# A hybrid attention and state-space layer: two attention gates computed by a third Strassen pair, and earlier steps around it

## Chip, cores and metric

The kernel runs on one core of a Trainium2 chip. The metric is the device time of one execution in microseconds (us); of the kernel before, three runs gave 857.27, 859.77 and 859.24 us, median 859.24. One further execution was taken by the hardware profiler; every row quoted below of the kernel before is from that one.

Engines are named as in the profile: PE is TensorE (matmuls), PEld its weight loads, DVE VectorE, ACT ScalarE, POOL GpSimd, SP the engine whose queue issues the DMAs. L259 is line 259 of the kernel.

## The reference

One layer works on T = 1088 tokens (1024 of a prompt, 64 of a sample) with a model width of 1024. One projection of the normalized input gives the queries, keys and values, two gates `z`, the state-space input `u`, and two merging gates `g`:

```python
xn = rmsnorm(h, norm_gain)
z = xn @ w_in
...
ya = (attn * jax.nn.silu(z_attn)) @ w_o_attn
ys = (ssm * jax.nn.silu(z_ssm)) @ w_o_ssm
merged = jax.nn.sigmoid(g_attn) * ya + jax.nn.sigmoid(g_ssm) * ys
h = h + merged @ w_out
h = h + jax.nn.sigmoid(h @ w_ple_gate) * (p @ w_ple_proj)
```

`attn` is a sliding-window attention, `ssm` a diagonal complex recurrence over the tokens with a gelu and a gated unit behind it. The change concerns `g_attn` (1024 columns of `w_in`, eight units of 128, called m = 0 to 7 here), `z_ssm` (four units), and the time at which the last rounds of the recurrence run.

## The kernel before

**Data.** Tiles hold 128 rows (features) by 1088 columns (tokens) in float32. Each float32 product is made of three matmuls (L259, L260, L261): both operands are split into a high and a low part (`hl_split`: ACT's copy L1158 and DVE's subtraction L162). 43 slots of SBUF are handed out and given back by the program as it is written; a step that needs a slot waits until the last reader of its former content is done. All loads and stores stand in SP's one queue, in program order.

**Clock.** PE's products are written out in one long order, and everything else hangs on a hand-made clock: `pump` is called once after each half of a plain product and once after each half of a Strassen product, and fires what `at(step, ...)` or `later(n, ...)` planned for that step. The tables `ROUND_AT`, `OUT_AT`, `BACK_AT`, `X_AT` and `RING_AT` are such steps. The framework then fixes the order in each engine; what is issued through `first` comes ahead of other work that is ready.

**Stages around the change** (steps in brackets):
- OA [120 to 144]: the last four output tiles of the attention product, four k each, three token blocks of 384, 384 and 320 (`BLK`). ACT copies them out of the banks (L173).
- Plain gates m = 4 to 7 [144 to 168]: eight k each over the same three blocks, so 72 matmuls a unit. DVE multiplies by the token scale RS, ACT takes tanh (L1339), DVE adds 1 and multiplies by the OA tile, and `pa_out` stores the result to DRAM.
- zB [168 to 196]: two pairs of units, each pair by a Strassen scheme (`seven`): seven products of four k over two halves of 544 tokens, in sub-blocks of 272 columns, so 7 x 4 x 3 x 2 = 168 matmuls a pair. `sink` adds the products up on ACT and DVE, and `z_late` finishes a half.
- gB [196 to 252]: four pairs, the same way; then the rest of the layer.

Strassen's products need sums of the quarters of x (S1 to S4 of the weights, T1 to T4 of x): `x_load` brings two tiles of x back from DRAM, three steps before `x_sums` scales them on ACT (L1304) and makes the sums and their splits on DVE and ACT; `x_t1` makes the last one's split later. The weights pass through a ring of four pieces: `rload` loads a unit of `w_in` into a slot, `make` splits a piece into the ring. `ring_start` begins that (steps 136 and 143).

**Rounds.** The recurrence runs in eight rounds of four groups. For a round r, `s_load` brings its inputs, `s_rot` makes a table of rotations (DVE and POOL, L728 among its lines), `s_wb` transposes on PE (L746) and has ACT copy the result out (L747), `s_state` makes the state's input on PE (L789), reading that copy, and rotates and scans it on DVE and POOL (L805), `s_state2` finishes the state (L825 to L827), and `s_out` makes the output on PE (L839, L840), which ACT copies (L841) and SP stores (L844). `ROUND_AT` plans `s_wb` and `s_state`, with the other parts at fixed distances, and `OUT_AT` plans `s_out`. `s_back` reads the output of a quarter of the rounds back for the gelu, at `BACK_AT`.

Of the kernel before, what the change touches and what calls it, by code (L numbers as in the profile page):

```python
# [16 lines left out]
AF = mybir.ActivationFunctionType  # L17
AX = mybir.AxisListType
MUL, ADD, SUB = ALU.mult, ALU.add, ALU.subtract
# [17 lines left out]
ENG = dict(tab="VG", e="V", cf="VG", rot="VG", r8="GGGV", unrot="VG", rotadd="VVG", rope="VVVG", ropeadd="GGV", ropec="VG",  # L37
           gelu="V", norm="V", w="V", gate="VG", glu="GGGV", mg="VVG", pa="V", h="V", acc="V",
           y="VVVG", z="V", ph="VVG", xs="V", ws="V", rs="VG", ms="V", hq="G", zz="GV", tcp="AV")
BACK_AT = (176, 186, 196, 206)  # L40
ROUND_AT = (32, 40, 50, 73, 86, 103, 121, 140)
OUT_AT = (41, 54, 62, 81, 98, 113, 137, 150)
SLOT = 1096
MANUAL = False
AHEAD = 400
BLK = [(0, 384), (384, 384), (768, 320)]
BLK2 = [(0, 416), (416, 416), (832, 256)]
HT = T // 2
RAWS = 3
RING_AT = (136, 143)  # L50
RING = 4
X_AT = (148, 151, 154, 158)

SEVEN = [("A11", "B11", "a", 1), ("A12", "B21", "b", 1), ("S2", "T2", "a", 0), ("S3", "T3", "c", 1),
         ("S1", "T1", "a", 0), ("S4", "B22", "a", 0), ("A22", "T4", "c", 0)]
# [79 lines left out]
def emit(nc, tc, a, es, dbg=None):  # L135
# [7 lines left out]
    S = Slots(sp, NSLOT)  # L143
# [7 lines left out]
    zb_dram = dp.tile([4, P, T], F32, name="zb_dram")  # L151

    V, G, A, PE, DMA = nc.vector, nc.gpsimd, nc.scalar, nc.tensor, nc.sync
# [13 lines left out]
    def stt(o, x, s, y, op0, op1):  # L167
        V.scalar_tensor_tensor(o, x, s, y, op0, op1)  # L168

    def first(f, *x, **k):  # L170

        with tc.high_priority(AHEAD):
            f(*x, **k)  # L173
# [7 lines left out]
    def ett(key, o, x, y, op):  # L181
        (nc.gpsimd if eng(key) == "G" else nc.vector).tensor_tensor(o, x, y, op)  # L182
# [36 lines left out]
    def wget():  # L219
        i = wi["get"]  # L220
        wi["get"] += 1
        if wi["split"] <= i:
            wsplit()
        if wi["split"] == i + 1:
            wsplit()
        return S.ap(whs[i % 2][0]), S.ap(whs[i % 2][1])
# [12 lines left out]
    def at(i, f, *args):  # L239
        plan.setdefault(i, []).append((f, args))  # L240
# [22 lines left out]
    def gemm(w, off, ops, blk, pumps=True):  # L263

        c0, cn = blk
        ps = gbank()[:, :cn]
        nk = len(ops)
        for k, (xh, xl) in enumerate(ops):
            ws = slice(off + P * k, off + P * k + P)
            mm3(ps, w[0][:, ws], w[1][:, ws], S.ap(xh)[:, c0:c0 + cn], S.ap(xl)[:, c0:c0 + cn],  # L270
                k == 0, k == nk - 1)
            if pumps and k == nk // 2 - 1:
                pump()
        if pumps:
            pump()
        return ps, slice(c0, c0 + cn)
# [6 lines left out]
    RS = S.ap(rsb)  # L283
# [378 lines left out]
    V, vtt, stt = V_, vtt_, stt_  # L662
# [212 lines left out]
    for r, b in enumerate(ROUND_AT):  # L875
# [5 lines left out]
        if r % 2:  # L881
            q = r // 2
            b = max(BACK_AT[q], OUT_AT[r])
# [15 lines left out]
    for m in (2, 3):  # L899
        uq[m] = S.alloc()  # L900
        w = wget()
        for b in BLK:
            ps, cs = gemm(w, 0, X, b)
# [209 lines left out]
    AG = [None] * 4  # L1113
# [22 lines left out]
    def pa_out(m, t):  # L1136
        DMA.dma_start(pa_dram[m], S.ap(t))
        S.free(t)

    for mp in range(2):  # L1140
        ts = [gate_unit() for _ in range(2)]
        w = wget()
        for m in (2 * mp, 2 * mp + 1):
            t = ts[m % 2]
            for b in BLK:
                ps, cs = gemm(w, 512 * (m % 2), AG, b)
# [31 lines left out]
    def plain(*units):  # L1178
        for u in units:
            i = len(raws)  # L1180
            raws.append(u)
            pieces.extend([("half", i, 0, ()), ("half", i, 1, (i,))])

    def pairs_of(units):
        n = len(units) // 2
        p = []
        for x in range(n):
            i = len(raws)
            raws.extend(units[2 * x:2 * x + 2])
            p.append([("half", i, 0, ()), ("half", i, 1, ()), ("S2", i, i + 1, ()), ("S3", i, i + 1, ()),  # L1190
                      ("S1", i, i + 1, ()), ("S4", i, i + 1, (i,)), ("half", i + 1, 1, (i + 1,))])
        pieces.extend(p[x][y] for x, y in order(n))
# [8 lines left out]
            o += [(x, 5), (x, 6)]  # L1201
        return o

    plain(*(a["w_in"][j] for j in range(22, 26)))
    pairs_of([a["w_in"][j] for j in range(14, 18)])
    pairs_of([a["w_in"][j] for j in range(26, 34)])
    plain(a["w_glu"][0], a["w_glu"][1], *(a["w_os"][j] for j in range(4)))
    plain(a["w_pp"][0], a["w_pp"][1])
# [64 lines left out]

    at(RING_AT[0], ring_start, 1)
    at(RING_AT[1], ring_start, RAWS)
    OA = []
    for m in range(4, 8):
        if m % 2 == 0:
            w = wget()
        OA.append(S.alloc_f())  # L1280
        for b in BLK:
            ps, cs = gemm(w, 512 * (m % 2), AG, b)
            first(A.activation, S.ap(OA[-1])[:, cs], ps, AF.Copy)
    for hl in AG:
        S.free(hl[0])
        S.free(hl[1])

    XP = {n: [None] * 4 for n in ("B11", "B21", "B22", "T1", "T2", "T3", "T4")}
    XS = {}
    for k in range(4):  # L1290
# [30 lines left out]

    for k, b in enumerate(X_AT):
        at(b - 3, x_load, k)
        at(b, x_sums, k)

    for hl in whs:
        S.free(hl[0])
# [1 line left out]
    k4 = [P * k for k in range(4)]  # L1329
    X8 = [(S.ap(h), S.ap(l)) for h, l in X]  # L1330
    ring.append(S.alloc())
    for m in range(4, 8):
        w2 = pget(2)
        t = S.alloc()
        for b in BLK:
            cs = slice(b[0], b[0] + b[1])
            ps = gemm2([(y, o) for y in w2 for o in k4], X8, b)
            first(vtt, S.ap(t)[:, cs], ps, RS[:, cs], MUL)
            A.activation(S.ap(t)[:, cs], S.ap(t)[:, cs], AF.Tanh, scale=0.5)  # L1339
        stt(S.ap(t), S.ap(t), 1.0, S.ap(OA[m - 4]), ADD, MUL)  # L1340
        S.free(OA[m - 4])
        pa_out(m, t)
# [3 lines left out]
    def seven(n, B, subs, sink, done=None):  # L1346


        st = {}
        for x, y in order(n):  # L1350
            _, bn, acc_, new = SEVEN[y]
            w, = pget(1)
            for s, (o, cn) in enumerate(subs):
                if new:
                    st[x, s, acc_] = gbank()[:, :cn]
                ps = st[x, s, acc_]
                for k in range(4):
                    ws = slice(P * k, P * k + P)
                    bh, bl = (z[:, o:o + cn] for z in B[bn][k])
                    mm3(ps, w[0][:, ws], w[1][:, ws], bh, bl, bool(new) and k == 0, k == 3, not new)  # L1360
                pump()
                sink(x, y, s, o, cn, ps, st.get((x, s, "c")))
            if done and x == n - 1:
                done(y)


    def quarters(dst, hw, full, late):


        last = {}  # L1370

        def q(x, r, hf):
            return lambda o, cn: dst(x, r)[:, hw * hf + o:hw * hf + o + cn]

        def sink(x, y, s, o, cn, ps, pc):
            def fin(r, hf, p):
                full(x, r, hf, o, cn, p)
                n = last[x, r, hf] = last.get((x, r, hf), 0) + cn
                if n == hw:
                    late(x, r, hf)  # L1380

            if y in (0, 2, 4):
                d = q(x, *((0, 0), None, (1, 0), None, (1, 1))[y])(o, cn)
                first(A.activation, d, ps, AF.Copy)
                if y == 4:
                    first(vtt, d, d, pc, ADD)
                    fin(1, 1, None)
            elif y == 1:
                d = q(x, 0, 0)(o, cn)
                first(vtt, d, d, ps, ADD)  # L1390
                fin(0, 0, None)
            elif y == 5:
                fin(0, 1, ps)
            elif y == 6:
                d = q(x, 1, 0)(o, cn)
                first(vtt, d, d, ps, ADD)
                fin(1, 0, None)

        return sink

    XSUB = [(0, HT // 2), (HT // 2, HT // 2)]
    ZB, GB = {}, {}
# [8 lines left out]
    def scaled(get):  # L1411
        def full(x, r, hf, o, cn, p):
            cs = slice(HT * hf + o, HT * hf + o + cn)
            if p is not None:
                first(vtt, get(x, r)[:, cs], p, RS[:, cs], MUL)
        return full

    ht = {}

    def z_late(x, r, hf):  # L1420
        cs = slice(HT * hf, HT * hf + HT)
        z = S.ap(ZB[x, r])[:, cs]
        if (r, hf) != (0, 1):
            ett("rs", z, z, RS[:, cs], MUL)
        t = S.alloc()
        A.activation(cut(t, HT), z, AF.Tanh, scale=0.5)
        stt(z, cut(t, HT), 1.0, z, ADD, MUL)
        S.free(t)
        n = ht[x, r] = ht.get((x, r), 0) + 1
        if n == 2:  # L1430
            DMA.dma_start(zb_dram[2 * x + r], S.ap(ZB[x, r]))
            S.free(ZB[x, r])

    def g_late(x, r, hf):
# [10 lines left out]
    for k in range(4):  # L1445
        later(k + 1, x_t1, k)
    get = tile_of(ZB)
    seven(2, XP, XSUB, quarters(get, HT, scaled(get), z_late))
    zb, pin = [], []

    def x_done(y):
# [22 lines left out]
    get = tile_of(GB)  # L1474
# [6 lines left out]
    for m in range(4):  # L1481
# [4 lines left out]
        for b in BLK:  # L1486
            cs = slice(b[0], b[0] + b[1])
            ps = gemm2([(w2[m % 2], o) for o in k4], Z2P, b)
# [47 lines left out]
    for m in range(8):  # L1536
# [4 lines left out]
        for b in BLK:  # L1541
            cs = slice(b[0], b[0] + b[1])
            ps = gemm2([(w2[m % 2], o) for o in k4], ZSP, b)
# [14 lines left out]
    for m in range(8):  # L1558
# [3 lines left out]
        for b in BLK:  # L1562
            cs = slice(b[0], b[0] + b[1])
            o = 256 * (m % 2)
            ps = gemm2([(w2[m % 4 // 2], o), (w2[m % 4 // 2], o + P)], PHP, b)
# [71 lines left out]
    RS = S.ap(S.alloc())  # L1637
# [60 lines left out]
    for i, (blks, m) in enumerate(steps):  # L1698
        if m < 4:
            w = pget(2)  # L1700
        elif i < 8:
            w = kept[m] = pget_kept()
        else:
            w = kept[m]
        pp_load(i + 1)
        pp = S.ap(pq[i])
        for ci in blks:
            b = BLK2[ci]
            t = S.ap(tmp[ntmp % 2])
            ntmp += 1  # L1710
            cs = slice(b[0], b[0] + b[1])
            ps = gemm2([(y, o) for y in w for o in k4], HHP, b)
# [5 lines left out]
            n = i % 8  # L1718
# [148 lines left out]
```

## Time and profile before

| | before |
|---|---|
| median of three runs | 859.24 us (857.27 to 859.77) |
| profiled execution, time | 859.96 us |
| profiled execution, span | 858.0 us |
| mean granted PE clock | 0.983 |
| stage OA, 351.23 to 382.40 us | 31.17 us |
| gates m = 4 and 5, to 408.13 us | 25.73 us |
| gates m = 6 and 7, to 432.03 us | 23.90 us |
| zB, two pairs, to 474.16 us | 42.13 us |
| gB, four pairs, to 558.38 us | 84.22 us |

The span is what the profiler saw of the engines, from the first instruction to the last; the time is what the runs are compared by. In the quoted rows an instruction group has its start, its length, engine, line, operation, output and inputs; brackets give the idle time of the engine before it and what ended that. The waits view sums such idle times by what ended them: total, number and longest.

### The profile page before, as it was taken

How to read it: one execution, taken by the hardware profiler on the slowest of the kernel's cores; microseconds unless marked ns; L12 is line 12 of the kernel's file. 1: busy time of each engine (PE TensorE's matmuls, PEld its weight loads, DVE VectorE, ACT ScalarE, POOL GpSimd, SP SyncE). 2: the span in 40 equal slices, each digit the busy share in tenths (PEclk: the TensorE clock that was granted, in tenths of full speed). 3: DMA queues.
4: the chain of work that ended last, by engine and by line, in shares of the span. 5: the costliest groups of instructions: out<-in, count | busy, mean ns of one | idle time of the engine just before them, and what ended most of it. 6: DMA issues, size and time to landing. Idle time of an engine off the chain costs nothing.

```text
span 858.0 us, 14478 instructions
## 1 busy us (share of the span) xinstructions
PE 835.6 (97%) x5575; PEld 800.2 (93%) x5575; DVE 625.3 (73%) x1242; ACT 355.8 (41%) x736; POOL 179.7 (21%) x203
## 2 busy tenths in 40 slices
PE   8999999899999999999999999999999999999994
PEld 7999999677778999999999999999999999999993
DVE  6897798667778777759689866888994657655473
ACT  8311211355553312236355544453446335454441
POOL 0178464100013233130000101140000222000051
PEclk9999999799999999999999999999999999999997
DMA  8431033310102253538432322494356321620135
GB/s 326 167 125 51 22 64 78 57 63 2 46 1 54 69 125 80 131 115 258 157 126 78 126 102 78 180 358 158 104 202 253 134 78 43 230 85 31 36 113 178
DMA packets 73989, 100.38 MB, mean 117 GB/s; under 512 B 38720, under 2 KB 53696, under 8 KB 73920
## 3 DMA queue, kind: packets, MB, share of 16 engines
q1 hardware_dynamic: 73776, 99.45, 35.3%
q8 instruction: 44, 0.72, 0.3%
q14 instruction: 25, 0.20, 0.1%
q10 hardware_dynamic: 144, 0.00, 0.0%
HBM read 74.31 MB, written 25.12 MB: 116 GB/s over the span
## 4 chain that ended last, share of the span: by engine, by line
PE 82%; DVE 8%; DMA 2%; issue 2%; ACT 2%; POOL 2%; SPq 0%; POOLq 0%; DVEq 0%; ACTq 0%
PE bank L259 25%; PE bank L261 24%; PE bank L260 24%; DVE s L182 2%; DVE s L162 2%; PE bank L1025 2%; PE bank L1079 2%; PE bank L1067 1%; POOL quad L182 1%; ACT s L1034 1%; PE bank L789 1%; POOL s L182 1%; DVE s L206 1%; DMA s<-w_out 1%; PE bank L388 1%
## 5 line engine op out<-in xcount | busy, mean ns | idle before, releaser
L259 PE MATMUL bank<-s,s 128*128 128x384 f32 (+4 forms) x1568 | 499.9, 319 | 3.4 <-DVE s L168 2.3
L261 PE MATMUL bank<-s,s 128*128 128x384 f32 (+4 forms) x1568 | 493.9, 315 | 0.0
L260 PE MATMUL bank<-s,s 128*128 128x384 f32 (+4 forms) x1568 | 493.8, 315 | 0.0
L259 PEld LDWEIGHTS bank<-s,s 128*128 128x128 f32 x1568 | 296.7, 189 | 10.6 <-issue 5.1
L261 PEld LDWEIGHTS bank<-s,s 128*128 128x128 f32 x1568 | 296.8, 189 | 0.8 <-issue 0.6
L260 PEld LDWEIGHTS bank<-s,s 128*128 128x128 f32 x1568 | 296.7, 189 | 0.6 <-issue 0.2
L162 DVE TENSOR_TENSOR s<-s,s 128x512 fp32r<-128x512 f32 (+3 forms) x167 | 121.4, 737 | 57.1 <-ACT s L1158 52.9
L182 POOL TENSOR_TENSOR s<-s,s 128x272 f32<-128x272 f32 (+5 forms) x60 | 71.5, 1195 | 310.2 <-DVE s L162 137.8
L1158 ACT ACTIVATE s<-s 128x512 fp32r<-128x512 f32 (+1 forms) x142 | 88.2, 632 | 81.7 <-PE bank L261 49.1
L182 DVE TENSOR_TENSOR s<-s,s 128x256 f32<-128x256 f32 (+5 forms) x160 | 101.9, 649 | 17.5 <-POOL s L182 7.7
L173 ACT ACTIVATE s<-bank 128x272 f32<-128x272 f32 (+4 forms) x111 | 46.7, 428 | 102.5 <-PE bank L261 102.2
L168 DVE SCALAR_TENSOR_TENSOR s<-s,s 128x416 f32<-128x416 f32 (+5 forms) x66 | 45.5, 701 | 39.1 <-ACT s L173 26.9
L204 ACT ACTIVATE s<-s 128x1024 fp32r<-128x1024 f32 (+5 forms) x38 | 35.2, 934 | 66.2 <-PE bank L261 49.8
L162 DVE TENSOR_TENSOR s<-bank,s 128x272 f32<-128x272 f32 (+3 forms) x105 | 46.5, 463 | 22.0 <-PE bank L261 10.9
L182 POOL TENSOR_TENSOR quad<-quad,s 128x272 f32<-128x272 f32 (+1 forms) x15 | 21.1, 1421 | 113.2 <-ACT s L173 110.3
L1034 ACT ACTIVATE s<-bank,at 128x192 f32<-128x192 f32 (+2 forms) x68 | 27.1, 410 | 29.5 <-DVE at L168 29.4
L206 DVE TENSOR_TENSOR s<-s,s 128x1024 fp32r<-128x1024 f32 (+3 forms) x30 | 33.8, 1137 | 6.9 <-ACT s L204 6.9
L1158 ACT ACTIVATE s<-quad 128x544 fp32r<-128x544 f32 x36 | 23.0, 656 | 28.2 <-DVE quad L182 27.6
L182 POOL TENSOR_TENSOR s<-s 128x256 f32<-128x256 f32 (+2 forms) x22 | 18.4, 841 | 62.5 <-DVE s L162 23.4
L165 POOL TENSOR_TENSOR rst<-rsw,mhalf 128x3 f32<-128x3 f32 (+4 forms) x7 | 5.6, 816 | 116.3 <-DVE rsw L378 116.3
L182 DVE TENSOR_TENSOR s<-s 128x256 f32<-128x256 f32 (+3 forms) x45 | 23.6, 534 | 6.3 <-POOL quad L182 2.7
L162 DVE TENSOR_TENSOR s<-quad,s 128x544 fp32r<-128x544 f32 x36 | 25.9, 742 | 1.2 <-ACT s L1158 1.2
(146 smaller groups left out, 738.4 us busy)
## 6 DMA issues: line engine op xcount, KB each, us to landing
s<-w_in SPq DMA_DIRECT2D x32, 512.0 KB
s<-x SPq DMA_DIRECT2D x19, 544.0 KB
s<-w_pg SPq DMA_DIRECT2D x12, 512.0 KB
pa_dram<-s SPq DMA_DIRECT2D x8, 544.0 KB
gb_dram<-s SPq DMA_DIRECT2D x8, 544.0 KB
quad<-gb_dram SPq DMA_DIRECT2D x8, 544.0 KB
s<-pa_dram SPq DMA_DIRECT2D x8, 544.0 KB
pp_dram<-quad SPq DMA_DIRECT2D x8, 544.0 KB
```

What stands on the lines that cost most here:

```text
L162: V.tensor_tensor(o, x, y, op)
L168: V.scalar_tensor_tensor(o, x, s, y, op0, op1)
L173: f(*x, **k)
L182: (nc.gpsimd if eng(key) == "G" else nc.vector).tensor_tensor(o, x, y, op)
L204: A.activation(f32r(h), x, AF.Copy, scale=1.0 if scale is None else scale)
L206: (G if on == "G" else V).tensor_tensor(f32r(l), x, h, SUB)
L259: PE.matmul(ps, f32r(wh), f32r(xl), start=first, stop=False, **k)
L260: PE.matmul(ps, f32r(wlo), f32r(xh), start=False, stop=False, **k)
L261: PE.matmul(ps, f32r(wh), f32r(xh), start=False, stop=last, **k)
L1025: PE.matmul(o, q, KTR[rows, 64 * n + 64 - nk:64 * n + 64], start=True, stop=True)
L1034: A.activation(pe[:, 64 + x * nk:64 + (x + 1) * nk], bank[3 + kv][:, jp * nk:(jp + 1) * nk], AF.Exp, bias=nm[:, x:x + 1], scale=0.125, acc ...
L1158: A.activation(f32r(hl[0]), raw, AF.Copy)
```

## The change

Two of attention's gates, m = 6 and 7, leave the plain loop and become the first of three pairs of the Strassen call that had zB's two. Their finishing (`a_late`) is called from `z_late` for pair 0: the same token scale, tanh, and multiplication by the OA tile as in the plain loop, by halves, and `pa_out` at the second half. The ring's list of pieces follows: two plain units and three pairs where there were four and two. The Strassen call thus starts at step 156, before at step 168, and ends at 198, before at 196.

The sums of x are planned three to six steps earlier, with their loads; since these loads now fall into OA, the code that defines and plans them moves ahead of OA's loop, unchanged. `RING_AT` goes from 136 to 137. Rounds 4 to 7, their outputs, and the four read-backs fire earlier. The lines below the move shift: the scaling of x is L1292 in the new kernel and L1304 in the old, its loads L1288 and L1300, the plain gates' tanh L1340 and L1339.

```diff
-BACK_AT = (176, 186, 196, 206)
-ROUND_AT = (32, 40, 50, 73, 86, 103, 121, 140)
-OUT_AT = (41, 54, 62, 81, 98, 113, 137, 150)
+BACK_AT = (172, 182, 192, 202)
+ROUND_AT = (32, 40, 50, 73, 84, 99, 114, 129)
+OUT_AT = (41, 54, 62, 81, 96, 109, 126, 144)
...
-RING_AT = (136, 143)
+RING_AT = (137, 143)
...
-X_AT = (148, 151, 154, 158)
+X_AT = (145, 147, 149, 152)
...
-    plain(*(a["w_in"][j] for j in range(22, 26)))
-    pairs_of([a["w_in"][j] for j in range(14, 18)])
+    plain(*(a["w_in"][j] for j in range(22, 24)))
+    pairs_of([a["w_in"][j] for j in (24, 25, 14, 15, 16, 17)])
...
-    for m in range(4, 8):
+    for m in range(4, 6):
         w2 = pget(2)
...
+    def a_late(r, hf):
+
+        cs = slice(HT * hf, HT * hf + HT)
+        z = S.ap(ZB[0, r])[:, cs]
+        if (r, hf) != (0, 1):
+            ett("rs", z, z, RS[:, cs], MUL)
+        A.activation(z, z, AF.Tanh, scale=0.5)
+        stt(z, z, 1.0, S.ap(OA[2 + r])[:, cs], ADD, MUL)
+        n = ht[4 + r] = ht.get(4 + r, 0) + 1
+        if n == 2:
+            S.free(OA[2 + r])
+            pa_out(6 + r, ZB[0, r])
+
     def z_late(x, r, hf):
+        if x == 0:
+            a_late(r, hf)
+            return
...
-            DMA.dma_start(zb_dram[2 * x + r], S.ap(ZB[x, r]))
+            DMA.dma_start(zb_dram[2 * x - 2 + r], S.ap(ZB[x, r]))
...
-    seven(2, XP, XSUB, quarters(get, HT, scaled(get), z_late))
+    seven(3, XP, XSUB, quarters(get, HT, scaled(get), z_late))
```

Where the instructions stand shows at three places. First ACT in OA, around the last round's copy L747 (the rows L1158 are the high parts of weight pieces, read from a slot that a load of `w_in` filled; L173 copies OA's product out; L841 copies out round 6's output). Before:

```order
L841 ACTIVATE s_162_3465<-bank_69 128x272
L841 ACTIVATE s_162_3465<-bank_70 128x272
L1158 ACTIVATE s_169_3579<-s_161_3457 128x512
L173 ACTIVATE quad<-bank_64 128x384
L747 ACTIVATE s_75_1114<-bank_69 128x512
L1304 ACTIVATE s_173_3613<-s_173_3613,gain 128x1088
```

In the new kernel:

```order
L841 ACTIVATE s_46_382<-bank_69 128x272
L841 ACTIVATE s_46_382<-bank_70 128x272
L1158 ACTIVATE s_166_3531<-s_168_3533 128x512
L1158 ACTIVATE s_167_3532<-s_168_3533 128x512
L173 ACTIVATE quad<-bank_64 128x384
L1292 ACTIVATE s_192_3741<-s_192_3741,gain 128x1088
L173 ACTIVATE quad<-bank_65 128x384
L747 ACTIVATE s_159_3261<-bank_69 128x512
```

L747 stood ahead of the first scaling of x, and now stands behind it and behind both splits of the first weight piece. Second, SP's queue ahead of that, with the loads which those read. Before:

```order
L173 DMA s_160_3451<-w_in 128x1024
L173 DMA s_161_3457<-w_in 128x1024
L1137 DMA pa_dram<-s_143_2905 128x1088
L844 DMA y_dram<-s_147_3062 8x16x136 x4
L688 DMA s_157_3307<-ssm_q 128x320
```

In the new kernel:

```order
L760 DMA s_74_1113<-t_dram 128x32x16
L691 DMA s_75_1114<-u_dram 128x1x136
L1137 DMA pa_dram<-s_151_3075 128x1088
L173 DMA s_168_3533<-w_in 128x1024
L1288 DMA s_192_3741<-x 128x1088
L844 DMA y_dram<-s_46_382 8x16x136 x4
L173 DMA s_174_3588<-w_in 128x1024
```

The first load of `w_in` for the ring stood ahead of round 5's output stores (the four L844 shown of before), and now stands directly ahead of round 6's, with the first load of x behind it. That load goes into the slot in which `s_rot` of round 7 had kept its temporary (`s_161_3414`). Third, DVE from round 6's scans (L805) to the end of its state (L827). Before:

```order
L805 SCALAR_TENSOR_TENSOR s_156_3306<-s_74_1113,s_156_3306 128x272 x2
L182 TENSOR_TENSOR s_155_3305<-s_156_3306,s_151_3222 128x272 x2
L162 TENSOR_TENSOR s_157_3307<-s_155_3305 64x2x136 x4
L182 TENSOR_TENSOR s_74_1113<-s_44_380,s_46_382 128x256
L825 COPY st<-s_157_3307 128x4
L826 COPY st<-s_157_3307 128x4
L182 TENSOR_TENSOR s_74_1113<-s_74_1113,s_153_3288 128x256
L827 COPY s_157_3307<-sm 128x4
```

In the new kernel:

```order
L168 SCALAR_TENSOR_TENSOR s_151_3075<-s_151_3075,bank_65 128x384
L805 SCALAR_TENSOR_TENSOR s_158_3260<-s_147_3007,s_158_3260 128x272
L182 TENSOR_TENSOR s_157_3259<-s_158_3260,s_46_382 128x272 x2
L168 SCALAR_TENSOR_TENSOR s_151_3075<-s_151_3075,bank_66 128x320
L162 TENSOR_TENSOR s_159_3261<-s_157_3259 64x2x136 x2
L206 TENSOR_TENSOR s_4_83<-s_152_3156,s_3_82 128x1024
L162 TENSOR_TENSOR s_159_3261<-s_157_3259 64x2x136 x2
L182 TENSOR_TENSOR s_147_3007<-s_44_380,s_46_382 128x256
L825 COPY st<-s_159_3261 128x4
L826 COPY st<-s_159_3261 128x4
L182 TENSOR_TENSOR s_159_3261<-s_159_3261,s_147_3007 128x256
L827 COPY s_159_3261<-sm 128x4
```

Between them now stand attention's last product being multiplied in (L168) and the low part of the last `w_oa` piece (L206, the subtraction of `split_to`). Round 7's table, which frees the load's slot, follows behind L827 in both kernels.

More of the change, by code (lines that the diff above doesn't have):

```diff
@@ L1275, in emit @@
     at(RING_AT[1], ring_start, RAWS)
-    OA = []
-    for m in range(4, 8):
[L1278 to L1286, printed above, removed]
     XP = {n: [None] * 4 for n in ("B11", "B21", "B22", "T1", "T2", "T3", "T4")}
@@ L1324, in emit @@
         at(b, x_sums, k)
+    OA = []
+    for m in range(4, 8):
+        if m % 2 == 0:
+            w = wget()
+        OA.append(S.alloc_f())
+        for b in BLK:
+            ps, cs = gemm(w, 512 * (m % 2), AG, b)
+            first(A.activation, S.ap(OA[-1])[:, cs], ps, AF.Copy)
+    for hl in AG:
+        S.free(hl[0])
+        S.free(hl[1])
     for hl in whs:
@@ L1331, in emit @@
     ring.append(S.alloc())
-    for m in range(4, 8):
+    for m in range(4, 6):
         w2 = pget(2)
```

## The prediction

> **What bounds the kernel now.** I read the page first: who is busy, and the chain that ended last.
>
> ```profile
> span 858.0 us, 14478 instructions
> PE 835.6 (97%) x5575; PEld 800.2 (93%) x5575; DVE 625.3 (73%) x1242; ACT 355.8 (41%) x736; POOL 179.7 (21%) x203
> PEclk9999999799999999999999999999999999999997
> PE 82%; DVE 8%; DMA 2%; issue 2%; ACT 2%; POOL 2%; SPq 0%; POOLq 0%; DVEq 0%; ACTq 0%
> ```
>
> TensorE (PE) is busy for 835.6 of 858.0 us and carries 82% of the chain, at full clock outside two slices. So a matmul taken away is worth its own time, and any other engine counts only where it makes PE wait. Next I read the stages that the change touches, from the windows view. Columns: the window, its length, then the busy time of PE, PEld, DVE, ACT and POOL, the granted clock, the DMA share and GB/s.
>
> ```profile
> 351.23:382.40 31.17, 30.99 (x218) 29.98 (x217) 19.43 (x51) 10.60 (x20) 8.09 (x8) 1.00 0.37 89
> 382.40:408.13 25.73, 25.73 (x162) 25.73 (x161) 23.70 (x41) 16.89 (x26) 2.13 (x2) 1.00 0.82 256
> 408.13:432.03 23.90, 23.90 (x147) 23.90 (x145) 16.18 (x25) 10.87 (x20) 0.00 (x0) 1.00 0.42 140
> 432.03:474.16 42.13, 42.13 (x339) 42.13 (x337) 36.63 (x59) 22.24 (x40) 3.65 (x2) 1.00 0.29 104
> 474.16:558.38 84.22, 84.22 (x675) 84.22 (x673) 61.73 (x89) 41.19 (x75) 13.02 (x8) 1.00 0.33 125
> ```
>
> In order: attention's output product (OA); the plain gates m = 4, 5; the plain gates m = 6, 7; zB in two Strassen pairs; gB in four. From 382.40 to 558.38 PE is busy in every microsecond. The windows begin and end at matmuls that the PE timeline shows, where the width of the streamed tile changes:
>
> ```profile
> 408.13 0.34 PE L259 MATMUL bank<-s,s 128*128 128x384 f32 x1
> 432.03 0.29 PE L259 MATMUL bank<-s,s 128*128 128x272 f32 x1
> 474.16 0.29 PE L259 MATMUL bank<-s,s 128*128 128x272 f32 x1
> ```
>
> **Part 1: two plain gates become a Strassen pair.** Gates 6 and 7 took 408.13 to 432.03, 23.90 us, for 2 x 72 = 144 matmuls: 166 ns each. They go. A pair is 7 products x 4 k x 3 matmuls x 2 halves = 168 matmuls, and two pairs took 42.13 us: 21.06 us a pair, 125 ns a matmul (gB agrees: 84.22 / 4 = 21.06). PE has no cover in any of these rows, so all of it is on the path: 21.06 - 23.90 = **-2.84 us**.
>
> [...]
>
> The work behind the new pair (`a_late`: tanh and a multiply by OA, then the store that fires from `pa_out`) is the same per gate as before, on DVE and ACT, which stood idle for 5.5 and 19.9 of the 42.13 us. It lies beside PE there, and costs nothing while DVE stays below its window; if that cover went, the last sums of a pair (some 1.2 us) would come late. The weight pieces rise from four to seven for these two units (seven splits on ACT and DVE), in the same two windows. I count both at 0, with 1.2 us as the other end (they shorten nothing on PE, so there is none below 0).
>
> **Part 2: rounds 4 to 7 and their read-back fire earlier.** The same matmuls, DMAs and DVE work are issued, only sooner, and PE's instructions keep their cost. What can be won is the wait that before shows in them, and what can be lost is a new one. The PE timeline shows the two last rounds (L789 starts a round's state), and the waits view of 340 to 600 us has one row:
>
> ```profile
> PE bank L789 <- ACT s L747: 0.2, 1, 0.2
> 355.88 1.15 PE L789 MATMUL bank<-s,s 128*64 128x136 f32 x16 [0.18 <-ACT s L747]
> 371.98 0.39 PE L839 MATMUL bank<-s,s 128*128 128x136 f32 x2
> 373.74 0.43 PE L259 MATMUL bank<-s,s 128*128 128x384 f32 x1
> 376.99 0.60 PE L746 MATMUL bank<-sm,s 128*128 128x128 f32 x4
> 378.23 0.42 PE L259 MATMUL bank<-s,s 128*128 128x384 f32 x1
> 378.94 1.15 PE L789 MATMUL bank<-s,s 128*64 128x136 f32 x16
> ```
>
> So at most **-0.18 us** is to be won (round 6); round 7's L789 at 378.94 waited for nothing. Now the loss. In the new order ACT's copy L747, which L789 of round 7 needs, stands behind the first weight piece's two L1158 and the first scaling of x (L1292), while before it stood ahead of the first scaling, with only one split of an already loaded weight near it. The L1158 wait for a w_in load; SP issues that load into a slot that DVE's rotation table of round 7 has to leave first; and that table stands on DVE behind all of round 6's state. I time the two arms from the start of round 6's L789.
>
> PE's arm, in the new order: L789 itself 1.07; 89 matmuls of 384 and 320 columns at 166 ns, 14.8; round 6's output (371.98 to 373.74), 1.8; round 7's L746 to L752 (376.99 to 378.23), 1.2. PE arrives after **18.9 us**.
>
> The other arm needs DVE, SP and ACT:
>
> ```profile
> 356.99 0.68 DVE L162 TENSOR_TENSOR s<-s,s 128x512 fp32r<-128x512 f32 x1
> 361.06 1.89 DVE L182 TENSOR_TENSOR s<-s,s 128x272 f32<-128x272 f32 x2
> 362.87 2.47 DVE L162 TENSOR_TENSOR s<-s 64x272 f32<-64x272 f32 x4
> 366.19 0.17 DVE L827 COPY s<-sm 128x4 f32<-128x4 f32 x1
> 368.27 0.24 DVE L728 COPY s<-s 128x16 f32<-128x16 f32 x2
> 384.80 1.35 DVE L182 TENSOR_TENSOR s<-s,s 128x272 f32<-128x272 f32 x2
> 386.08 1.78 DVE L162 TENSOR_TENSOR s<-s 64x272 f32<-64x272 f32 x4
> 353.45 1.22 DVE L206 TENSOR_TENSOR s<-s,s 128x1024 fp32r<-128x1024 f32 x1
> 343.71 0.55 DVE L168 SCALAR_TENSOR_TENSOR s<-s,bank 128x384 f32<-128x384 f32 x1
> ```
>
> Round 6 ran on DVE from 355.88 to L827 at 366.19: 10.3 us, a 512-wide split of 0.68 among it. In the new order that split is gone and three L168 (0.5 each) and one L206 (1.22) stand in it: 10.3 - 0.7 + 2.7 = 12.3. With round 7's speeds for the two groups of L182 and L162 (1.35 and 1.78 where round 6 shows 1.89 and 2.47) it is 11.1. From L827 to the table's last writes I take four of the six L182 that lie between 366.19 and 368.27, with the copies 1.6 us. The load can be issued after 12.7 to 13.9 us.
>
> ```profile
> 377.93 0.34 SPq L1300 DMA_DIRECT2D s<-x  x1
> 370.09 0.63 ACT L1158 ACTIVATE s<-s 128x512 fp32r<-128x512 f32 x1 [3.44 <-POOL s L182]
> 377.08 0.47 ACT L173 ACTIVATE quad<-bank 128x384 f32<-128x384 f32 x1
> 377.62 0.60 ACT L747 ACTIVATE s<-bank 128x512 f32<-128x512 f32 x1
> 381.70 1.21 ACT L1304 ACTIVATE s<-s,gain 128x1088 f32<-128x1088 f32 x1 [3.48 <-DMA s<-x]
> ```
>
> A load issued at 377.93 released ACT at 381.70, 3.77 us later. Then ACT has two L1158, L173, the scaling (L1304, now L1292), L173 and L747: 2 x 0.63 + 2 x 0.47 + 1.21 + 0.60 = 4.0, about 3.7 since one starts some 0.07 before the last ends. L747 ends after 20.2 to 21.4 us, PE is there after 18.9: a wait of 1.3 to 2.5. Its bounds by rows are 0 (round 7 before) and 3.48 (the wait at 381.70, which now stands ahead of L747). I take **+1.6 us**, toward the faster DVE rows, since round 7's own row shows them. Behind the waiting L789 stands everything on PE, in order, so the wait counts in full.
>
> **Part 3: sums of x sooner, RING_AT 136 to 137.** The same scalings, DVE sums and eight loads, three to six steps sooner: partly into OA, where DVE has 11.7 of 31.2 us free, partly into the gates, where it had 2.0 of 25.7 free. Four gates of cover have become two. PE needs the sums first at the new pair's third product, 2 x 3.0 us into it, and before they were fed through 16.18 of 23.90 us of DVE work that is no longer there to overlap. I count 0; bounds: 0, and 3 us if the sums slip by as much as ACT waited for one load (3.48).
>
> **Sum** against the profiled execution (859.96 us, span 858.0): -2.84 - 0.18 + 1.6 = -1.4, so 858.5. The median of the runs shown, 859.24, lies 0.72 below that execution; so I state **857.8 us**.
>
> **The rivals.**
>
> - *No new wait.* DVE or POOL leaves the slot sooner, or the load lands sooner than 3.77 us. For it: round 7's L789 waited for nothing at 378.94. Against: three more L168 and one L206 in round 6's stretch. Then -3.0: 856.2 us. It takes a new wait below some 0.4 us to be faster by over 0.3% (2.6 us; about what a measurement here can tell from no change).
> - *The wait halves the clock (the other side).* One place, round 7's L789: if the w_in load or x's lands late, PE stands for 3.5 us or more and the granted clock falls, as it did once before:
>
> ```profile
> 152.00:155.00 3.00, 0.00 (x0) 0.00 (x1) 1.55 (x8) 2.40 (x11) 0.00 (x0) 1.00 0.00 0
> 155.88:159.29 3.41, 3.41 (x15) 2.43 (x12) 2.27 (x8) 0.00 (x0) 0.82 (x1) 0.50 0.32 37
> 159.29:162.70 3.41, 3.41 (x13) 2.53 (x12) 1.37 (x4) 0.10 (x1) 0.36 (x1) 0.50 0.74 49
> 162.70:166.12 3.42, 3.42 (x15) 3.35 (x14) 3.38 (x9) 1.77 (x9) 1.28 (x2) 0.50 0.06 12
> ```
>
> After 3.00 us without PE the clock stood at 0.50 for three windows, 10.24 us: work worth 5.1 us was lost. That gives -3.0 + 3.5 + 5.1 = +5.6: 864.8 us; with one such window +2.2. It decides from a wait of about 3 us on. Against it: my own arms give 1.3 to 2.5. [...]
> - *DVE is full in the two gates left.* It was busy 23.70 of 25.73 us there. If the pieces or sums for the pair come late, PE waits at its start: +1 to +3 us on top, 858.8 to 860.8.
> - *The change doesn't do what it says*: the pair is paced by its weight pieces, so that it costs what two gates cost: -0.18 + 1.6, 860.7 us.
>
> **How the numbers follow.** Forecast (the pair's gain less a wait of 0.5 to 2.5) 0.50; no new wait 0.26; halved clock 0.12; DVE full 0.08; no gain 0.04. Faster by over 0.3%: no new wait, 0.26. Slower by over 0.3% (above 861.8): the halved clock 0.12, and a part of the last two and of the forecast's upper tail (a wait near 3 with a cover of part 1 or 3 gone), 0.08: 0.20. The same: 0.54. The range runs from 855.2 (full gain, and 1 us of waits that I don't see going) to 862.8 (a 3.5 us wait with one or two halved windows); what lies beyond it is about 0.2.
>
> **What would show it.** The 144 matmuls at 166 ns gone and 168 at 125 in their place, before zB's; L789 <- ACT L747 in the waits with 1.3 to 2.5 us at one instance, the last round; the wait ahead of that L747 on ACT put to the DMA from w_in; no clock below 1.00 around it; no PE wait at the new pair. Wrong would be: a wait of PE elsewhere, above all on DVE at the third product; a wait near 0; or a granted clock of 0.50 in OA.

## The result, and the profile after

The changed kernel is slower, by 0.7%. Six runs of it have the median 863.89 us (862.33 to 866.7), six of the kernel before 857.83 us (856.46 to 859.77); the ratio is 1.0073, with a 95% interval of 1.0056 to 1.0090. In a second comparison it was 1.0056 (1.0038 to 1.0074). By the medians it loses 6.1 and 5.2 us where I had forecast a gain of 1.4. (One slip in the part on the change: the plain gates' tanh keeps its line, L1339.)

The page of the changed kernel's profiled execution, which took 866.7 us:

```profile
span 864.9 us, 14548 instructions
PE 836.5 (97%) x5599; PEld 799.3 (92%) x5599; DVE 631.9 (73%) x1255; ACT 358.4 (41%) x743; POOL 181.5 (21%) x204
PE 73%; DVE 11%; DMA 5%; ACT 4%; issue 3%; POOL 3%; SPq 0%; POOLq 0%; DVEq 0%; ACTq 0%
```

PE's idle time rose from 22.4 to 28.4 us, and its share of the chain fell from 82% to 73%. Its busy time did not fall by the pair's 2.84 us either: in the window at half clock below, 12 matmuls count as 3.40 us of it, where 21 do at full clock in a second trace of this kernel, and in the seven pairs it counts 148.71 us, where 7 x 21.06 is 147.42. The PE timeline of this kernel shows which waits are larger or new (those of the first 160 us and of the last 40 stand in both kernels):

```profile
273.92 0.34 PE L789 MATMUL bank<-s,s 128*64 128x136 f32 x2 [2.03 <-ACT s L747]
372.09 0.34 PE L789 MATMUL bank<-s,s 128*64 128x136 f32 x2 [1.25 <-ACT s L747]
470.39 0.39 PE L259 MATMUL bank<-s,s 128*128 128x272 f32 x1 [0.56 <-ACT s L173]
489.65 0.39 PE L259 MATMUL bank<-s,s 128*128 128x272 f32 x1 [0.55 <-ACT s L173]
588.57 0.44 PE L259 MATMUL bank<-s,s 128*128 128x384 f32 x1 [1.45 <-DVE s L168]
590.19 0.45 PE L259 MATMUL bank<-s,s 128*128 128x384 f32 x1 [0.83 <-DVE s L168]
```

They are round 3 (0.78 before), round 7 (none before), two copies out of the banks in the pairs (none before), and the end of the gated unit behind gB (none before). The windows view of the same kernel adds the clock behind round 3's wait (the column behind POOL's), the new pair by itself, and the seven Strassen pairs as a whole:

```profile
275.30:278.70 3.40, 3.40 (x12) 3.40 (x11) 3.40 (x12) 0.00 (x0) 0.00 (x0) 0.50 0.26 63
412.21:433.30 21.09, 21.09 (x171) 21.09 (x170) 18.87 (x28) 12.84 (x26) 2.33 (x1) 1.00 0.38 130
412.21:562.04 149.83, 148.71 (x1178) 147.82 (x1177) 112.88 (x172) 73.04 (x134) 18.29 (x10) 1.00 0.35 124
```

From these the difference of the two profiled executions, 866.70 - 859.96 = 6.74 us, can be put together:

| where | us |
|---|---|
| round 3's wait, 2.03 for 0.78 | +1.25 |
| the window at half clock behind it, 3.41 x 0.5 (estimate) | +1.7 |
| rounds 6 and 7, 1.25 for 0.18 | +1.07 |
| two gates become a pair | -2.84 |
| seven pairs in 149.83, at 21.06 each 147.42 | +2.41 |
| the end of the gated unit, 1.45 + 0.83 | +2.28 |
| sum | +5.87 |

Of the remaining 0.9, some 0.2 lies ahead of round 3, whose wait began at 271.89 for 271.66 before, and some 0.6 beside the two waits at the end of the gated unit. The waits behind that are partly shorter and partly longer than before, and nearly cancel.

**Round 7** went as foretold. SP and ACT of the changed kernel; round 6's L789 began at 351.33:

```profile
364.89 0.33 SPq L173 DMA_DIRECT2D s<-w_in  x1
368.27 1.15 ACT L1158 ACTIVATE s<-s 128x512 fp32r<-128x512 f32 x2 [1.86 <-DMA s<-w_in]
371.45 0.59 ACT L747 ACTIVATE s<-bank 128x512 f32<-128x512 f32 x1
```

The load was issued 13.6 us after round 6's start (I had 12.7 to 13.9), ACT's copy ended after 20.7 (20.2 to 21.4), and PE, which stood idle for 1.25 us until 372.09, was there after 19.5 (18.9).

**Round 3** was not in my sum at all. First DVE and ACT of the kernel before, then of the changed one:

```profile
268.29 1.21 DVE L206 TENSOR_TENSOR s<-s,s 128x1024 fp32r<-128x1024 f32 x1
269.42 1.28 DVE L168 SCALAR_TENSOR_TENSOR s<-s,s 128x1088 f32<-128x1088 f32 x1
270.80 1.11 ACT L204 ACTIVATE s<-s 128x1088 fp32r<-128x1088 f32 x1 [1.92 <-DVE s L168]
271.81 0.58 ACT L747 ACTIVATE s<-bank 128x512 f32<-128x512 f32 x1
```

```profile
268.52 0.72 DVE L182 TENSOR_TENSOR s<-s 128x256 f32<-128x256 f32 x1
269.17 0.68 DVE L728 COPY s<-s 128x16 f32<-128x16 f32 x2
269.77 1.21 DVE L206 TENSOR_TENSOR s<-s,s 128x1024 fp32r<-128x1024 f32 x1
270.90 1.28 DVE L168 SCALAR_TENSOR_TENSOR s<-s,s 128x1088 f32<-128x1088 f32 x1
272.28 1.11 ACT L204 ACTIVATE s<-s 128x1088 fp32r<-128x1088 f32 x1 [3.18 <-DVE s L168]
273.29 0.58 ACT L747 ACTIVATE s<-bank 128x512 f32<-128x512 f32 x1
```

Two lines are new on DVE: an L182 and the two L728, part of round 4's rotation table. It was planned two steps earlier (83 for 85), and so came to stand ahead of an L206 and an L168 on which an ACT split waits, and behind that split stands round 3's copy L747. 1.25 us of DVE's work appear again as 1.25 us of PE's waiting.

### The profile page after: what moved, and what is told of

Same layout as the page of the kernel before. It is cut to its first block, busy times and chain, and to the rows that moved or that the text cites. A ratio compares the mean times of both kernels' runs of the same rounds, so it can differ in the third digit from the quotient of the medians.

```text
span 864.9 us, 14548 instructions
## 1 busy us (share of the span) xinstructions
PE 836.5 (97%) x5599; PEld 799.3 (92%) x5599; DVE 631.9 (73%) x1255; ACT 358.4 (41%) x743; POOL 181.5 (21%) x204
## 4 chain that ended last, share of the span: by engine, by line
PE 73%; DVE 11%; DMA 5%; ACT 4%; issue 3%; POOL 3%; SPq 0%; POOLq 0%; DVEq 0%; ACTq 0%
PE bank L259 22%; PE bank L261 21%; PE bank L260 21%; DVE s L182 3%; DVE s L162 3%; DVE s L168 2%; PE bank L1025 2%; PE bank L1079 2%; PE bank L1067 1%; POOL s L182 1%; DMA s<-x 1%; POOL quad L182 1%; PE bank L789 1%; ACT s L1034 1%; DMA s<-p 1%
## 5 line engine op out<-in xcount | busy, mean ns | idle before, releaser
L259 PE MATMUL bank<-s,s 128*128 128x272 f32 (+4 forms) x1576 | 501.9, 319 | 6.3 <-DVE s L168 4.6
L260 PE MATMUL bank<-s,s 128*128 128x272 f32 (+4 forms) x1576 | 494.9, 314 | 0.0
L261 PE MATMUL bank<-s,s 128*128 128x272 f32 (+4 forms) x1576 | 494.9, 314 | 0.0
L259 PEld LDWEIGHTS bank<-s,s 128*128 128x128 f32 x1576 | 298.6, 190 | 15.4 <-DVE s L168 5.9
L162 DVE TENSOR_TENSOR s<-s,s 128x512 fp32r<-128x512 f32 (+3 forms) x170 | 123.4, 737 | 52.8 <-ACT s L1158 48.9
L182 POOL TENSOR_TENSOR s<-s,s 128x272 f32<-128x272 f32 (+5 forms) x61 | 73.6, 1210 | 317.4 <-DVE s L162 121.4
L182 DVE TENSOR_TENSOR s<-s,s 128x256 f32<-128x256 f32 (+5 forms) x166 | 105.6, 647 | 19.1 <-POOL s L182 5.5
L1158 ACT ACTIVATE s<-s 128x512 fp32r<-128x512 f32 (+1 forms) x145 | 89.6, 631 | 72.5 <-PE bank L261 41.4
L173 ACT ACTIVATE s<-bank 128x272 f32<-128x272 f32 (+4 forms) x117 | 48.6, 426 | 100.3 <-PE bank L261 100.2
L168 DVE SCALAR_TENSOR_TENSOR s<-s,s 128x416 f32<-128x416 f32 (+5 forms) x66 | 45.6, 703 | 43.9 <-ACT s L173 27.0
L162 DVE TENSOR_TENSOR s<-bank,s 128x272 f32<-128x272 f32 (+3 forms) x101 | 44.5, 460 | 22.9 <-PE bank L261 11.9
L182 POOL TENSOR_TENSOR quad<-quad,s 128x272 f32<-128x272 f32 (+1 forms) x15 | 21.2, 1424 | 112.2 <-DMA quad<-x 89.8
L206 DVE TENSOR_TENSOR s<-s,s 128x1024 fp32r<-128x1024 f32 (+3 forms) x30 | 34.9, 1171 | 6.9 <-ACT s L204 6.9
L1158 ACT ACTIVATE s<-quad 128x544 fp32r<-128x544 f32 x36 | 23.1, 656 | 27.6 <-DVE quad L182 27.0
L182 DVE TENSOR_TENSOR s<-s 128x256 f32<-128x256 f32 (+3 forms) x45 | 25.8, 588 | 8.3 <-DMA s<-w_in 3.2
L182 POOL TENSOR_TENSOR s<-s 128x256 f32<-128x256 f32 (+2 forms) x22 | 18.3, 834 | 62.8 <-DVE s L162 23.6
```

The lines of the kernel that those rows point to most:

```text
L162: V.tensor_tensor(o, x, y, op)
L206: (G if on == "G" else V).tensor_tensor(f32r(l), x, h, SUB)
L259: PE.matmul(ps, f32r(wh), f32r(xl), start=first, stop=False, **k)
L260: PE.matmul(ps, f32r(wlo), f32r(xh), start=False, stop=False, **k)
L261: PE.matmul(ps, f32r(wh), f32r(xh), start=False, stop=last, **k)
L1158: A.activation(f32r(hl[0]), raw, AF.Copy)
```

## The experiments

Each comparison has its own runs of the kernel before, on the same chip.

**Round 4's table moved.**

```diff
-            at(b + OFF[x], f, r)
+            at(b + OFF[x] + (-4 if (x, r) == ("rot", 4) else 0), f, r)
```

> The changed kernel with one edit: the rotation table of round 4 is planned at step 79 instead of 83, where it takes another slot and stands on DVE behind round 3's state instead of ahead of the work that frees ACT for round 3's copy L747. Theory (round 4's table delays round 3): round 3's L789 waits about 1.1 us or less instead of 2.03, the granted clock stays at 1.00 there, and the time falls by 2 to 3 us against the changed kernel (861 to 862). Rival (that wait is a chance of one execution): the same time as the changed kernel within 1 us, and the same wait.

860.92 us, 1.0024 (1.0010 to 1.0038) of before, some 3 us under the changed kernel's medians. Round 3 waited less, though more than I expected, since one L182 of the table stayed ahead, and the matmuls of 384 columns behind it followed one another at 0.17 to 0.18 us, where in the changed kernel's window at 0.50 they stand 0.32 apart:

```profile
274.26 0.34 PE L789 MATMUL bank<-s,s 128*64 128x136 f32 x2 [1.43 <-ACT s L747]
```

**Round 4 alone, in the kernel before.**

```diff
-ROUND_AT = (32, 40, 50, 73, 86, 103, 121, 140)
-OUT_AT = (41, 54, 62, 81, 98, 113, 137, 150)
+ROUND_AT = (32, 40, 50, 73, 84, 103, 121, 140)
+OUT_AT = (41, 54, 62, 81, 96, 113, 137, 150)
```

> The kernel before with round 4 alone moved (ROUND 86 to 84, OUT 98 to 96). Theory: round 3's L789 waits 2 us instead of 0.78, the clock is halved for one window, and the kernel is 2.5 to 3 us slower than before. Rival (it takes the other moves too): no difference above 0.8 us.

862.73 us against 858.58, 1.0035 (1.0015 to 1.0055). Its PE timeline, and its windows view:

```profile
272.99 0.34 PE L789 MATMUL bank<-s,s 128*64 128x136 f32 x2 [2.03 <-ACT s L747]
```

```profile
274.60:278.00 3.40, 3.40 (x13) 3.40 (x11) 3.40 (x12) 0.00 (x0) 0.00 (x0) 0.51 0.28 66
```

A move of one round by two steps costs 3.0 us by the ratio (1.3 to 4.7 by its interval), with no other part of the change: the same wait, and the same half clock, which together make 1.25 + 1.7 = 2.95 (1.7 by the estimate above). The rival falls. This trace has two more waits that before lacks, of 0.34 us at 344.25 and 1.19 at 374.02; what they add to the median was not measured.

**The pair alone**: the changed kernel with all five tables of before.

> The changed kernel with all five tables of before (rounds, outputs, read-backs, ring, sums): the third pair alone. Theory: rounds 3 and 6 wait 0.78 and 0.18 as before, round 7 not at all; the pair gives -2.84 us, and what the late sums of x and the fuller DVE make PE wait at the pairs comes on top, 1 to 5 us; so -1.8 to +2 us against before. Rival (the pair's gain is lost in the pair itself): PE takes over 22.5 us for each of the three pairs, and no wait shows.

858.25 us against 858.58, 0.9995 (0.9981 to 1.0010): no difference that can be told. Rounds 3, 6 and 7 waited 0.78, 0 and 0 in its trace; what is new is one wait for the late sums of x, in the first pair:

```profile
416.12 0.40 PE L259 MATMUL bank<-s,s 128*128 128x272 f32 x1 [1.01 <-DVE s L162]
```

The pair's gain is there, but smaller: the seven pairs took 148.98 us (406.05 to 555.03), and the two gates and six pairs of before 150.25 (23.90 + 126.35): a gain of 1.3 us, which the interval allows. The wait came 9.06 us after the pairs' start, so ahead of the fourth product. To win the rest, the sums of x must come sooner.

**The sums sooner, the rounds of before.** The pair alone with X_AT 147, 149, 152, 155.

> The third pair with before's rounds, outputs, read-backs and ring, and with X_AT 147, 149, 152, 155 (between before's and the changed kernel's). Theory (the pair alone lost 1.0 us to late sums at its third product, and nothing else): that wait goes or halves, no wait shows at rounds 6 and 7, and the time is 1.5 to 2.5 us below before. Rival (the sums, moved into OA, push the copies of OA or of round 7 late): a new wait of 0.5 us or more there, and no gain against the pair alone.

Not as expected: 860.40 us, 1.0016 (1.0001 to 1.0031), slower rather than faster. Its PE, SP and ACT:

```profile
416.37 0.39 PE L259 MATMUL bank<-s,s 128*128 128x272 f32 x1 [1.66 <-ACT s L173]
421.30 0.39 PE L259 MATMUL bank<-s,s 128*128 128x272 f32 x1 [1.90 <-DVE s L162]
...
402.08 0.40 SPq L1288 DMA_DIRECT2D s<-x  x1
402.57 1.20 SPq L844 DMA_DIRECT2D y_dram<-s  x2
403.82 0.53 SPq L1288 DMA_DIRECT2D s<-x  x1
...
406.18 1.21 ACT L1292 ACTIVATE s<-s,gain 128x1088 f32<-128x1088 f32 x1 [1.80 <-DMA s<-x]
410.28 1.21 ACT L1292 ACTIVATE s<-s,gain 128x1088 f32<-128x1088 f32 x1 [1.80 <-DMA s<-x]
```

The last loads of x stand in SP's queue between and behind round 7's output stores, which can't be issued before round 7 is done; ACT waits 1.80 twice, and PE 1.66 and 1.90. The mean granted clock of its profiled execution was 0.979, that of the pair alone's 0.986. With round 7 at its old place, planning the sums earlier does not make them early. That is what the moved rounds are good for.

**The changed kernel again.**

> The changed kernel once more, beside the others on one chip, with a second trace. Theory (the 2.3 us of waits at the end of the gated unit hang on how late one load lands in an execution, while the waits of rounds 3 and 7 and of ACT's copies in the pairs are fixed by the order): L789 waits 2.0 and 1.25 again, the copies about 2 us again, and the two waits on DVE L168 are absent or under 1 us. Rival (those waits are fixed by the order too): they show 2 us again.

863.78 us, 1.0056 (1.0038 to 1.0074). Its profiled execution was the fastest of the six, 860.49. Rounds 3 and 7 and the copies waited again, the end of the gated unit did not, and the clock stayed at full speed behind round 3's wait. Its PE timeline, its windows view, and its waits from 260 to 830 us:

```profile
272.22 0.34 PE L789 MATMUL bank<-s,s 128*64 128x136 f32 x2 [2.03 <-ACT s L747]
...
368.60 0.34 PE L789 MATMUL bank<-s,s 128*64 128x136 f32 x2 [1.03 <-ACT s L747]
```

```profile
273.60:277.00 3.40, 3.40 (x21) 3.40 (x20) 3.40 (x12) 0.00 (x0) 0.00 (x0) 1.00 0.22 60
```

```profile
PE bank L259 <- ACT s L173: 1.4, 3, 0.6
```

The waits that the order fixes come back in each trace; the half clock and the gated unit's wait belong to some executions.

**zb's loads earlier**: `zb`'s four loads moved from `y == 4` to `y == 3` in `x_done`.

> The changed kernel with the four loads of zb_dram issued one product group earlier (after the fourth product of gB's last pair instead of the fifth). Theory (the two waits on DVE L168 at the end of the gated unit, 2.3 us, come from zb's first load landing 6.2 us after its issue where it took 4.1 before): DVE's first multiply no longer waits for it and 1.5 to 2.3 us are won against the changed kernel. Rival (that stretch is bound by the loads of p and the order on ACT): the two waits stay above 1.5 us and the time is the same within 0.7 us.

862.16 us, 1.0032 (1.0014 to 1.0051), and no wait at the end of the gated unit. But the changed kernel showed none either in its second trace, and no other variant of it showed more than 0.30 there, so this doesn't tell whether the edit removed anything. Undecided.

**Round 7's copy ahead of the scaling of x**: the changed kernel with X_AT 146, 148, 150, 152.

> The changed kernel with X_AT 146, 148, 150, 152 instead of 145, 147, 149, 152: ACT's copy L747 of round 7 then stands ahead of the first scaling of x. Theory (round 7's L789 waits by ACT's row of work behind the w_in load): its wait falls from 1.25 to 0.0 to 0.3 us, and the time by about 1.1 us. Rival (the load itself decides): the wait stays above 0.8 us.

862.27 us, 1.0041 (1.0021 to 1.0062), beside 863.78 for the changed kernel: 1.5 less, which the intervals do not separate. The trace shows the wait gone: round 7's L789 no longer waits, and round 3's does:

```profile
273.24 0.34 PE L789 MATMUL bank<-s,s 128*64 128x136 f32 x2 [2.03 <-ACT s L747]
370.08 0.34 PE L789 MATMUL bank<-s,s 128*64 128x136 f32 x2
```

**The read-backs of before**: the changed kernel with BACK_AT 176, 186, 196, 206.

> The changed kernel with the read-backs of before (BACK_AT 176, 186, 196, 206). Theory (the gelu steps L855 and L861 on ACT and L168 on DVE, put into the third pair and gB's first, hold up the copies that free PE's banks there): the waits on ACT L173 around 470 and 490 us, 1.1 us, and the stretching beside them, another 1.2, mostly go; 1 to 2 us are won. Rival (the weight pieces and their loads are what comes late there): those waits stay within 0.3 us of 1.1.

860.77 us, 1.0023 (1.0004 to 1.0042), 3.0 below the changed kernel, though the two intervals overlap a little; I had expected 1 to 2. The waits view from 260 to 830 us has no row for the copies L173 into `s` before L259 any more (1.4 in the changed kernel's second trace):

```profile
PE bank L789 <- ACT s L747: 3.2, 2, 2.0
PE bank L388 <- ACT s L173: 0.5, 1, 0.5
PE bank L259 <- DVE s L168: 0.3, 1, 0.3
```

and the seven pairs, from the first of these two marks of its PE timeline to the second, took 147.62 us, 0.2 over seven times 21.06:

```profile
406.72 0.29 PE L259 MATMUL bank<-s,s 128*128 128x272 f32 x1
...
554.34 0.34 PE L259 MATMUL bank<-s,s 128*128 128x384 f32 x1
```

It holds in the other traces too: the seven pairs took 149.6 to 150.3 us in the five with the moved read-backs (the changed kernel twice, round 4's table moved, zb's loads earlier, X_AT 146), and 147.6 to 148.3 in the three with the old ones (this one and the last two below). What stood in the way is seen on ACT of the changed kernel, ahead of the copies for which PE waited at 470.39:

```profile
468.43 1.10 ACT L861 ACTIVATE s<-s 128x1088 f32<-128x1088 f32 x1
469.43 0.62 ACT L1158 ACTIVATE s<-s 128x512 fp32r<-128x512 f32 x1
469.95 0.67 ACT L173 ACTIVATE s<-bank 128x272 f32<-128x272 f32 x2
```

L861 is a gelu's tanh, four steps sooner than before, and 1.1 us long.

**Three mends, and two of them.** The first kernel is the changed one with

```diff
-BACK_AT = (172, 182, 192, 202)
+BACK_AT = (176, 186, 196, 206)
...
-X_AT = (145, 147, 149, 152)
+X_AT = (146, 148, 150, 152)
...
-            at(b + OFF[x], f, r)
+            at(b + OFF[x] + ({"e": 2, "rot": -4}.get(x, 0) if r == 4 else 0), f, r)
```

and the second leaves the last edit out.

> The changed kernel with three mends at once: read-backs of before, X_AT 146, 148, 150, 152, and of round 4 alone s_e planned two steps later and s_rot four steps earlier, so that DVE's row of work ahead of round 3's state is that of before. Theory (three new waits took the pair's gain: round 3's, round 7's, and ACT's copies in the pairs): round 3 waits 0.78, round 7 under 0.3, the pairs nothing, no halved clock at round 3; the pair's 2.8 us are left, and the kernel is 1.5 to 2.8 us faster than before, 4.5 to 7 faster than the changed one. Rival (something else of the moved rounds costs time too): no faster than before within 1 us.

> The same without the mend of round 4: read-backs of before and X_AT 146, 148, 150, 152 alone. Theory: round 3 waits 2.0 again, which halves the clock in part of the executions; 1.3 (wait alone) to 3 us slower than the kernel with all three mends. Rival (round 3's wait is taken back later): within 0.8 us of it.

All three: 855.56 us against 858.97, **0.9961 (0.9944 to 0.9977)**, faster than both kernels. Two: 858.68, 0.9996 (0.9984 to 1.0008), 3.1 slower than all three. The waits of PE from 260 to 830 us with three mends, and round 3 with two:

```profile
PE bank L789 <- ACT s L747: 0.8, 1, 0.8
PE bank L388 <- ACT s L173: 0.5, 1, 0.5
PE bank L259 <- ACT s L173: 0.2, 1, 0.2
```

```profile
273.72 0.49 PE L789 MATMUL bank<-s,s 128*64 128x136 f32 x2 [2.03 <-ACT s L747]
```

With the three new waits gone, 3.4 us are won (2.0 to 4.8 by the interval), a range in which the pair's 2.84 lies. In this trace the seven pairs took 147.90 us (406.31 to 554.21), 2.35 less than the two gates and six pairs of before. The moved rounds without the pair were not run, so a small part of the gain may be theirs.

## Why the prediction was wrong

- **What bounds the kernel, and the pair's -2.84**: right. PE is the bound (busy for 97% of the span in both profiles), and the pair's gain appears once its surroundings are mended. The new pair took 21.09 us, where I had 21.06.
- **Round 7, +1.6**: right in place, mechanism and nearly in size. 1.03 to 1.35 in the five traces that had it, so below the 1.3 to 2.5 of my arms in most; putting L747 ahead of the scaling removed it.
- **"So at most -0.18 us is to be won ... Now the loss"**: this is the step that failed. I looked for the loss of the moved rounds at the rounds themselves, and at the last one only. Round 4's move by two steps I counted as nothing. Its table went past work on DVE that belongs to round 3, which is not moved. The row was there to be read: round 3 already waited 0.78 for the same copy, so every DVE instruction put ahead of it had to show. It cost 1.25 us in each of seven traces, and 3.0 and 3.1 us in time in the two direct comparisons; 1.25 and one window at half clock (1.7 by estimate), which followed in the traces of both, make 2.95.
- **"I count both at 0, with 1.2 us as the other end"** (DVE and ACT in the pairs): failed too. I summed their busy times over the stage and found room; but PE waited for single copies out of its banks on ACT (0.56 us at 470.39), and a gelu moved four steps forward stood ahead of them (L861, 1.10 us). The seven pairs took 2.4 us more than their matmuls; the old read-backs brought that back. The read-backs I had named among the moved parts, and given no term. Of the 6.74 us between the two profiled executions, round 3 with its half clock makes 2.95 and the pairs 2.4; my sum had both at 0.
- **Part 3, sums of x at 0**: right. There was no wait at the new pair's third product, as forecast. With the rounds left where they were it would not have been 0: 1.01 ahead of the fourth product, or 1.66 and 1.90 ahead of the third and the fourth.
- **The halved clock** I had as a rival, at round 7 and from a wait of about 3 us on. It came at round 3, behind 2.03 us in five of seven traces. The rival's price for one window (1.7) goes with the two direct comparisons; its place was wrong, and no run shows the 3 us, which were my estimate from the 3.00 us without PE. I had read that the clock fell "once before" and stood full outside two slices; a slice that shows 9 can hide a window at half clock: the first slice of before, 0 to 21.45, shows 9 with a mean of 0.92. The kernel before had one behind a wait of 2.02 us near its start, at 0.50 from 12.52 to 15.93, as its PE timeline and its windows view let one see (0.75 is the mean of 10 to 15 us):

```profile
11.31 0.44 PE L259 MATMUL bank<-s,s 128*128 128x384 f32 x1 [2.02 <-DVE s L168]
10.00:15.00 5.00, 3.69 (x15) 3.69 (x16) 5.00 (x7) 5.00 (x8) 0.00 (x0) 0.75 1.04 422
```

- **Not settled**: the 2.28 us at the end of the gated unit, in one of two traces of the changed kernel and in none of its six variants above 0.30. There DVE waited 2.69 us for zb's first load, and the executions' spread (860.5 to 866.7) leaves room for it in more of them; which part of the medians it makes was not measured.

## What to carry to other kernels

A step that was planned earlier was paid for here by what it passed in its engine's queue (round 4's table on DVE: 1.25 us of round 3's wait); look ahead of its new place, at what already waits there, and not only at the step itself. Room in an engine's busy time over a stage said nothing here about one copy that stood behind a long instruction (L861's 1.10 us on ACT, 0.56 of PE's waiting). And where a change moves several tables, each can be undone alone: here one pair's gain showed in the time only after three of its companions were put right.

## What the runs showed of the hardware

A wait of PE of 2.03 us, in the middle of a full stretch, came with a halved clock in five of the seven profiled executions that had it, and with none in two (the changed kernel again, at 1.00 from 273.60 to 277.00, and the read-backs of before). In the changed kernel the granted clock was 0.50 from 275.29 to 278.70, 3.41 us, and in round 4 alone 0.51 from 274.60 to 278.00. In X_AT 146, zb's loads earlier and two mends the PE timeline shows it by the spacing of the matmuls of 384 columns: 0.32 us behind the wait, as in the changed kernel's window, where it is 0.17 behind that window, and 0.17 to 0.18 behind the wait in the read-backs of before. A wait of 1.43 (round 3, round 4's table moved) was followed by a spacing of 0.17 to 0.18, one of 1.25 (round 7, the changed kernel) by a clock of 1.00. I had expected the fall from about 3 us on. Here 2 us were often enough, and the same wait in the same place costs 2.0 us in one execution and, with 1.7 us for one window (my estimate, 3.41 x 0.5), 3.7 or more in another.

Why one execution pays and another does not was not shown. The halved clock did not begin at one distance behind the wait: in zb's loads earlier and two mends round 3's 16 L789 themselves took 2.08 us, where they take 1.15 at full clock, while in the changed kernel the clock fell 1.37 us after the wait's end. Within the traces of before and of the changed kernel the falls lie whole multiples of 3.41 us apart (12.52, 36.41 and 155.88 in before: 7 and 35 times; 155.82 and 275.29 in the changed kernel: 35 times).

Such windows also fall where the change does nothing: both of these traces have 3.41 us at 0.50 from 12.5 and again from 36.4 us, and 10.24 us, three times as much, from 155.82 and 155.88. Ahead of the one at 36.41 in before the PE timeline shows no wait for 20 us. Each costs up to 1.7 us by the same estimate. Single executions of one kernel differed by several microseconds: of the kernel before, on one chip, one took 854.73 us at a mean granted clock of 0.989 and another 860.97 at 0.982.
